# Latent attention: GpSimd subtracts the low halves of the later heads' and the first output projection's weights

## The chip, the cores and the metric

The kernel runs on one core of one Trainium2 chip. A core has a matrix engine (TensorE, PE in the profile, with its weight loads as PEld), three engines for elementwise work (VectorE as DVE, ScalarE as ACT, GpSimd as POOL) and SyncE (SP), which here issues most of the loads. The metric is the device time of one execution in microseconds, taken as the median of several runs. Each engine executes its own instructions strictly in the order in which the program lists them; between engines, semaphores make an instruction wait for the results that it reads and for the buffers that it overwrites.

## The reference

A trunk of two layers on 512 tokens of width 1024, all in float32. Layer 0 mixes with multi-head latent attention (MLA), layer 1 with gated linear attention (GLA); each is followed by an MLP. The change lies in the attention of layer 0. Cut to what matters:

```
h = rms_norm(x) @ w_in                       # latents: 384 for q, 256 for k and v, 64 rotary
q  = rms_norm(c_q)  @ w_uq                   # 8 heads of 128 plain + 64 rotary columns
kv = rms_norm(c_kv) @ w_ukv                  # 8 heads of 128 key columns + 128 value columns
s  = (q_nope k_nope^T + q_rope k_rope^T) * scale, causal
o  = softmax(s) @ v                          # for each head
x  = x + concat(o) @ w_o
```

## The kernel before, in words

Every large product is computed from numbers that are split in two: `hi` is the number rounded to float32r, the form in which TensorE multiplies in one pass, and `lo` is what the rounding left. A product then takes three matmuls (`mm3`, lines 132 to 134): hi by hi, hi by lo, lo by hi. So each piece of weights, once loaded into a buffer `wraw`, costs one ScalarE copy with rounding (`wh`, line 124) and one VectorE subtraction `wl = wraw - wh` (line 127) before TensorE may use the low part. The function `piece` does this; `split` inside it already takes the engine of the subtraction as an argument.

The attention loops over eight heads. `project(h)` makes the plain part of q and k of head h: every fourth head it loads the weights of four heads (three loads `wraw_qn`, two loads `wraw_kn`, lines 580 and 584) and splits the key weights of all four (1024 columns); every second head it splits the query weights of two heads (768 columns). `scores(h)` forms the causal scores and the softmax, `turn` transposes the probabilities and splits them into PTh and PTl (lines 746 and 747), `values` multiplies by v. The loop runs them skewed: in the turn of head h it projects head h+2, transposes h, scores h+1 and multiplies h. The rotary halves of the queries of heads 4 to 7 are computed in the turns of heads 0 and 1 (`rotate_q(t, 1)`): of each such rotation GpSimd does one multiplication (line 624, four in all) and VectorE the rest (lines 623, 625, 626). In the turn of head 6 `out_start` splits the first 256 columns of w_o in two pieces of 1024 and begins the first output projection with heads 0 to 3.

The order of the instructions on each engine is not the order of the code: a scheduler sets it from the dependencies and its own estimates of costs. `afterwards()` asks that the splits of the later heads are issued after line 606 of head 1 (`started`). The buffers limit it too: `wraw` has 2, `wh` and `wl` have 4 each, so a load into `wraw` waits until both halves of the previous piece in that buffer have been formed, and SP issues its loads in order.

In the rows of the order below, a number behind a name is the buffer's own; the profile leaves it out. `wh_879`/`wl_880` are the query weights of heads 2 and 3, `wh_1160`/`wl_1161` the key weights of heads 4 to 7, `wh_1164`/`wl_1165` and `wh_1436`/`wl_1437` the query weights of heads 4, 5 and 6, 7, and `wl_1689`, `wl_1694` the two pieces of w_o. `qh_715`, `kh_728` belong to head 0, `qh_755`, `kh_768` to head 1; `set_773` to `set_776` are the rotated queries of the four token tiles, `tmp_913`, `tmp_919`, `tmp_1048` and `tmp_1054` what GpSimd multiplies for their second half.

Of the kernel before, what the change touches and what calls it, by code (L numbers as in the profile page):

```python
# [18 lines left out]
P = 128  # L19
# [3 lines left out]
ND = D // P  # L23
# [27 lines left out]
def trunk_kernel(ctx: ExitStack, tc: tile.TileContext, t_in: dict, out: bass.AP):  # L51
    nc = tc.nc
    PE, ACT, DVE, POOL, SP = nc.tensor, nc.scalar, nc.vector, nc.gpsimd, nc.sync
# [5 lines left out]
    def uname(s):  # L59
        count[0] += 1  # L60
        return f"{s}_{count[0]}"
# [14 lines left out]
    def bank(tag):  # L76
        return psum["pool"].tile([P, 512], F32, tag=f"ps_{tag}", bufs=psum["banks"][tag], name=uname("ps"))
# [41 lines left out]
    def f(ap):  # L119
        return ap.bitcast(F32)  # L120

    def split(src, hi, lo, hi_eng=ACT, lo_eng=DVE, order=lambda i: i):
        if hi_eng is ACT:
            order(ACT.activation(hi, src, AF.Copy))  # L124
        else:
            hi_eng.tensor_copy(hi, src)
        lo_eng.tensor_tensor(lo, src, f(hi), ALU.subtract)  # L127
# [29 lines left out]
    W_ROOM, W_AT = 1152, 128  # L157
    AT_UP = (124, 60)

    def room_for(tag, a, n, at=W_AT):  # L160
        t = sb.tile([P, W_ROOM], F32R, tag=tag, bufs=4, name=uname(tag))
        return t[:, at : at + a * n].rearrange("p (a n) -> p a n", a=a)

    def piece(raw, a, n, order=lambda i: i, at=(W_AT, W_AT)):
        hi = room_for("wh", a, n, at[0])
        lo = room_for("wl", a, n, at[1])
        split(raw, hi, lo, order=order)
        return hi, lo

    def cut(pair, *idx):  # L170
        return tuple(t[idx] for t in pair)
# [212 lines left out]
    def a_type(psum, w, x, start=True, stop=True, cols=slice(None)):  # L384
        nk = len(x)
        for k in range(nk):
            mm3(psum, cut(w, slice(None), k, cols), x[k], start and k == 0, stop and k == nk - 1)
# [9 lines left out]
    def col_chunk(w2d, c0, n):  # L397
        return load(w2d[:, c0 : c0 + n].rearrange("(k p) n -> p k n", p=P), w2d.shape[0] // P, n)


    def mla(layer, nrm, first, pools):
# [3 lines left out]
        X = nrm.out  # L405
# [34 lines left out]
        raw = sb.tile([P, ND, 256], F32, tag="wraw", bufs=2, name=uname("wraw"))  # L440
# [5 lines left out]
        for j in range(2):  # L446
            p = bank("c")
# [11 lines left out]
        raw = col_chunk(w_in, 256, P)  # L459
        w = piece(raw, ND, P)  # L460
        p = bank("b")
# [5 lines left out]
        raw = col_chunk(w_in, QL + KL, ROPE)  # L467
# [3 lines left out]
        p = bank("b")  # L471
# [23 lines left out]
        raw = sb.tile([P, 2, MH, VD], F32, tag="wraw", bufs=2, name="wraw_v")  # L495
# [18 lines left out]
        for t in range(NT):  # L514
            tk = slice(t * P, (t + 1) * P)
            for hf in range(2):
                p = bank("bc"[hf])
# [15 lines left out]
            if t == 1:  # L533
# [3 lines left out]
                for j in range(2):  # L537
                    y = tmp()
                    DVE.scalar_tensor_tensor(y, pkv[j], gcol("kvn", 2 * layer + j), r_kv, ALU.mult, ALU.mult)
                    hi, lo = (keep.tile([P, S], F32R, tag=f"ckv{j}{x}", name=f"ckv{j}{x}") for x in "hl")  # L540
# [16 lines left out]
        raw = sb.tile([P, 3, MH, ROPE], F32, tag="wraw", bufs=2, name="wraw_qr")  # L557
# [8 lines left out]
        for t in range(NT):  # L566
            tk = slice(t * P, (t + 1) * P)
            p = bank("b")
# [5 lines left out]
        wn, wk = {}, {}  # L574

        def project(h, tag="a"):
            if h % 4 == 0:
                raw = sb.tile([P, 3, 4, NOPE], F32, tag="wraw", bufs=2, name=uname("wraw_qn"))
                for k in range(3):
                    SP.dma_start(raw[:, k], w_uq[:, k, h : h + 4, :NOPE])  # L580
                wn["raw"] = raw
                raw = sb.tile([P, 2, 4, NOPE], F32, tag="wraw", bufs=2, name=uname("wraw_kn"))
                for k in range(2):
                    SP.dma_start(raw[:, k], w_ukv[:, k, h : h + 4, :NOPE])
                with afterwards():
                    wk["p"] = piece(raw.rearrange("p k h c -> p k (h c)"), 2, 512)
            if h % 2 == 0:
                raw = wn["raw"][:, :, h % 4 : h % 4 + 2, :].rearrange("p k h c -> p k (h c)")
                with afterwards():
                    wn["p"] = piece(raw, 3, 256)  # L590
            res = []
            for name, w, c, X_ in (("q", wn["p"], (h % 2) * P, CQ), ("k", wk["p"], (h % 4) * P, CKV)):
                p = bank(tag)
                a_type(p, w, X_, cols=slice(c, c + P))

                c0 = P if name == "q" else 0
                full = keep.tile([P, P], F32, tag=name + "f", bufs=2, name=uname(name + "f"))
                hi, lo = (keep.tile([P, S - c0], F32R, tag=name + x, bufs=2, name=uname(name + x)) for x in "hl")
                if name == "q":
                    ACT.activation(hi, p[:, c0:], AF.Copy, scale=SCALE)  # L600
                    ACT.activation(full, p[:, :P], AF.Copy, scale=SCALE)
                    DVE.scalar_tensor_tensor(lo, p[:, c0:], SCALE, f(hi), ALU.mult, ALU.subtract)
                else:
                    ACT.activation(hi, p, AF.Copy)
                    ACT.activation(full, p[:, :P], AF.Copy)
                    last = DVE.tensor_tensor(lo, p, f(hi), ALU.subtract)
                res.append((hi, lo, full))
            if h == 1:
                started.append(last.ins)
            return res  # L610
# [4 lines left out]
        def afterwards():  # L615
            return tc.issue_after(started[0]) if started else nullcontext()
# [4 lines left out]
        def rotate(dst, src, c, s, shape, eng=DVE):  # L621
# [12 lines left out]
            (P, NT, 2, H),  # L634
        )
        proj = {0: project(0)}


        p = bank("c")[:ROPE]
# [15 lines left out]
        def rotate_q(t, g):  # L655
            rotate(
                QR[t][:, g],
                qs[t].rearrange("p (g h a c) -> p g h a c", g=2, h=HH, a=2)[:, g],
                cos_q[:, t].unsqueeze(1).unsqueeze(1).to_broadcast([P, HH, 2, H]),
                sin_q[:, t].unsqueeze(1).unsqueeze(1).to_broadcast([P, HH, 2, H]),  # L660
                (P, HH, 2, H),
                POOL if g else DVE,
            )


        def turn_q(h):
            p = bank("c")
            for t in range(NT):
                tr(p[:, t * P : (t + 1) * P], QR[t][:, h // HH, h % HH : h % HH + 2].rearrange("p h a c -> p (h a c)"))
            for r in range(2):  # L670
                own, other = slice(r * ROPE, (r + 1) * ROPE), slice((1 - r) * ROPE, (2 - r) * ROPE)
                y = QST[h + r] = slot("B")
                ACT.activation(y[own], p[own], AF.Copy)
                DVE.tensor_tensor(y[other], p[own], f(y[own]), ALU.subtract)
# [54 lines left out]
        O = [None] * MH  # L729
# [25 lines left out]
        def values(h, PT):  # L755
            o = bank("c")
            for j in range(NT):
                vs = slice((h % 4) * VD, (h % 4 + 1) * VD)
                if j < NT - 1:
                    mm3(o[:, j * P :], cut(V[j][h // 4], slice(None), vs), PT[j], j == 0, False)  # L760
                else:
                    PE.matmul(o[:, j * P :], V[j][h // 4][:, vs], PT[j], start=False, stop=True)
            hi, lo = slot("B"), slot("B")
            ACT.activation(hi, o, AF.Copy)
            DVE.tensor_tensor(lo, o, f(hi), ALU.subtract)  # L765
            O[h] = (hi, lo)
# [3 lines left out]
        for h in range(MH):  # L770
            if h + 2 < MH:
                proj[h + 2] = project(h + 2)
            if h < 2:
                with afterwards():
                    for t in (2 * h, 2 * h + 1):
                        rotate_q(t, 1)
            elif h == 2:
                for r in range(HH, MH, 2):
                    turn_q(r)
            if h == MH - 2:  # L780
                begun = out_start(t_in["mla_w_o"][layer], O, 4)
            PT = turn(probs)
            if h + 1 < MH:
                probs = scores(h + 1, *proj[h + 1])
            values(h, PT)
# [2 lines left out]
        return O, begun  # L788


    def out_start(w2d, X, n, tags="aa"):
        raws, w, ps_ = [], [], []
        for m, tag in enumerate(tags):
            if m % 2 == 0:
                raws.append(col_chunk(w2d, m * P, 256))
            w.append(piece(raws[-1][:, :, m % 2 * P : (m % 2 + 1) * P], ND, P))
            ps_.append(bank(tag))

        taken = [0]

        def mms(n=ND):
            for k in range(taken[0], n):
                for p, w_ in zip(ps_, w):
                    mm3(p, cut(w_, slice(None), k), X[k], k == 0, k == ND - 1)
            taken[0] = n

        mms(n)
        return ps_, raws, mms
# [889 lines left out]
    for k0, k1 in ((0, 1), (1, 2), (2, 4), (4, 6), (6, 8)):  # L1698
        w = piece(raw0[:, k0:k1], k1 - k0, KL, tc.keep_in_program_order)
# [9 lines left out]
    O, begun = mla(0, nrm, w0, mla_pools)  # L1709
# [25 lines left out]
    Y, begun = gla(0, n_mix1, "B", "B")  # L1735
# [61 lines left out]
```

## Time and profile before

| What | us |
|---|---|
| Median of 3 runs | 1039.3 (1038.52 to 1039.54) |
| Profiled execution, its own time | 1039.79 |
| Its span in the profile | 1038.1 |
| TensorE busy | 1028.9 (99% of the span) |
| VectorE busy | 879.2 (85%) |
| ScalarE busy | 694.4 (67%) |
| GpSimd busy | 92.7 (9%) |
| Chain of waits: share of TensorE | 92% |
| Chain of waits: share of VectorE | 4% |

The attention's heads lie between about 60 and 150 us of the span. A row of the timeline reads: start, duration, engine, line, operation, output and inputs with their shapes, how many were merged, and in brackets how long the engine had been idle before and what ended that. Matmuls overlap: the next one starts before the profile ends the last, so the distance between starts is what one costs.

### The profile page before, as it was taken

The page shows a single profiled execution, that of the slowest core. Times are in us where ns is not written, and L with a number is a line of the kernel's source. Part 1 is how long each engine was busy: PE and PEld are TensorE (multiplying, and loading weights), DVE is VectorE, ACT ScalarE, POOL GpSimd, SP SyncE. Part 2 cuts the span into 40 slices and gives each one's busy share as a digit, 9 for nine tenths or more (in the row PEclk, how much of TensorE's full clock was granted, in tenths as well). Part 3 has the DMA queues.
Part 4 walks back from the last instruction along what each step waited for, and adds up shares of the span by engine and source line. Part 5 has one row for each costly group of instructions (what it writes and reads, how often), then busy time and mean ns, then how long its engine had stood idle before and what let it go on. Part 6 is the DMA issues. An engine that isn't in the chain of part 4 may idle for free.

```text
span 1038.1 us, 16859 instructions
## 1 busy us (share of the span) xinstructions
PE 1028.9 (99%) x6522; PEld 923.0 (89%) x6522; DVE 879.2 (85%) x1343; ACT 694.4 (67%) x1130; POOL 92.7 (9%) x128
## 2 busy tenths in 40 slices
PE   9999999999999999999999999999999999999997
PEld 7788888899999999998888888888989989989986
DVE  7889976999989989989686399469799999898994
ACT  7667754676776776786445566565677687677784
POOL 7400000400001101000000000000000001100000
PEclk9999999999999999999999999999999999999999
DMA  7501214777677777623312222164568777777422
GB/s 230 127 22 41 73 50 140 205 194 207 189 198 209 169 205 200 157 84 122 90 42 85 91 69 75 48 165 148 144 196 201 189 196 201 192 193 186 121 82 82
DMA packets 63169, 145.85 MB, mean 140 GB/s; under 512 B 9488, under 2 KB 32016, under 8 KB 60528
## 3 DMA queue, kind: packets, MB, share of 16 engines
q1 hardware_dynamic: 52928, 113.57, 33.8%
q0 software_dynamic: 8064, 29.36, 16.4%
q10 hardware_dynamic: 2096, 1.84, 0.6%
q8 instruction: 51, 0.84, 0.3%
q14 instruction: 30, 0.25, 0.1%
HBM read 142.39 MB, written 2.10 MB: 139 GB/s over the span
## 4 chain that ended last, share of the span: by engine, by line
PE 92%; DVE 4%; ACT 2%; DMA 1%; issue 1%; ACTq 0%; SPq 0%; DVEq 0%
PE ps L987 25%; PE ps L1007 13%; PE ps L1000 13%; PE ps L132 10%; PE ps L133 10%; PE ps L134 10%; PE ps L1175 2%; PE ps L149 1%; PE ps L1429 1%; PE ps L1209 1%; PE ps L436 1%; PE ps L1556 1%; DVE wl L127 1%; ACT wh L124 1%; PE ps L1479 0%
## 5 line engine op out<-in xcount | busy, mean ns | idle before, releaser
L124 ACT ACTIVATE wh<-wraw 128x1024 fp32r<-128x1024 f32 x139 | 146.1, 1056 | 113.7 <-PE ps L133 38.4
L127 DVE TENSOR_TENSOR wl<-wraw,wh 128x1024 fp32r<-128x1024 f32 x139 | 169.7, 1222 | 36.5 <-ACT wh L124 35.8
L987 PE MATMUL ps<-T,wh 128*128 128x256 f32 x896 | 154.7, 275 | 0.1
L127 DVE TENSOR_TENSOR wl<-comb,wh 128x1024 fp32r<-128x1024 f32 x112 | 136.6, 1221 | 14.4 <-ACT wh L124 14.4
L124 ACT ACTIVATE wh<-comb 128x1024 fp32r<-128x1024 f32 x112 | 118.6, 1059 | 43.3 <-issue 30.0
L987 PEld LDWEIGHTS ps<-T,wh 128*128 128x128 f32 x896 | 135.0, 188 | 0.4 <-ACT tmp L1017 0.3
L987 PE MATMUL ps<-T,wl 128*128 128x256 f32 x448 | 123.3, 275 | 0.0
L1007 PE MATMUL ps<-wh,set 128*128 128x512 f32 x392 | 122.1, 390 | 0.0
L987 PE MATMUL ps<-set,wh 128*128 128x256 f32 x672 | 116.9, 276 | 0.0
L132 PE MATMUL ps<-set,wh 128*128 128x512 f32 x280 | 109.6, 391 | 0.0
L133 PE MATMUL ps<-set,wh 128*128 128x512 f32 x280 | 109.5, 391 | 0.0
L134 PE MATMUL ps<-set,wl 128*128 128x512 f32 x280 | 109.2, 390 | 0.0
L1000 PE MATMUL ps<-hidden_parts,wh 128*128 128x256 f32 x784 | 105.8, 275 | 0.0
L987 PEld LDWEIGHTS ps<-set,wh 128*128 128x128 f32 x672 | 101.9, 188 | 0.5
L1000 PEld LDWEIGHTS ps<-hidden_parts,wh 128*128 128x128 f32 x784 | 96.6, 188 | 0.0
L987 PE MATMUL ps<-set,wl 128*128 128x256 f32 x336 | 92.5, 275 | 0.0
L1007 PEld LDWEIGHTS ps<-wh,set 128*128 128x128 f32 x392 | 73.6, 188 | 15.2
L987 PEld LDWEIGHTS ps<-T,wl 128*128 128x128 f32 x448 | 84.1, 188 | 0.0
L1007 PE MATMUL ps<-wl,set 128*128 128x512 f32 x196 | 76.3, 389 | 0.0
L987 PEld LDWEIGHTS ps<-set,wl 128*128 128x128 f32 x336 | 63.1, 188 | 0.0
L134 PEld LDWEIGHTS ps<-set,wl 128*128 128x128 f32 x280 | 52.6, 188 | 11.0
L133 PEld LDWEIGHTS ps<-set,wh 128*128 128x128 f32 x280 | 52.6, 188 | 10.9 <-DVE set L765 0.2
(406 smaller groups left out, 2189.5 us busy)
## 6 DMA issues: line engine op xcount, KB each, us to landing
comb<-in_mlp_w_down_dram SPq DMA_DIRECT2D x74, 512.0 KB, 4.2
wraw<-in_mlp_w_up_dram SPq DMA_DIRECT2D x18, 1024.0 KB, 4.9
wraw<-in_mlp_w_up_dram SPq DMA_DIRECT2D x28, 512.0 KB, 5.7
comb<-in_mlp_w_down_dram POOLq DMA_DIRECT2D x28, 512.0 KB, 7.5
wraw<-in_gla_w_in_dram SPq DMA_DIRECT2D x12, 1024.0 KB, 5.1
comb<-in_mlp_w_up_dram SPq DMA_DIRECT2D x14, 512.0 KB, 4.7
comb<-in_mlp_w_up_dram POOLq DMA_DIRECT2D x14, 512.0 KB, 6.7
wraw<-in_mlp_w_up_dram POOLq DMA_DIRECT2D x14, 512.0 KB, 7.3
```

Of the source, the lines that this page charges most:

```text
L124: order(ACT.activation(hi, src, AF.Copy))
L127: lo_eng.tensor_tensor(lo, src, f(hi), ALU.subtract)
L132: PE.matmul(psum, wh, xh, start=start, stop=False)
L133: PE.matmul(psum, wh, xl, start=False, stop=False)
L134: PE.matmul(psum, wl, xh, start=False, stop=stop)
L149: PE.transpose(psum, src, ident[: src.shape[0], : src.shape[0]])
L436: PE.matmul(p, w[:, i, j * P : (j + 1) * P], x, start=start, stop=stop)
L987: PE.matmul(o, a_, x_, start=start and j == 0 and k == 0 and n == 0, stop=k == KH - 1 and n == 2, skip_group_check=True)
L1000: PE.matmul(o, w_[:, k, j * P : (j + 1) * P], x_[:, ts], start=opens, stop=k == 1 and n == 2, skip_group_check=True)
L1007: PE.matmul(o, x_, w_, start=start and k == 0 and n == 0, stop=k == 1 and n == 2, skip_group_check=True)
L1175: PE.matmul(p, a, x, start=k == 0 and n == 0, stop=k == 3 and n == 2)
L1209: PE.matmul(o, a, b_, start=False, stop=k == 3 and n == 2, skip_group_check=True)
```

## The change

`piece` gets an argument `lo_eng` and hands it to `split`. For the key weights of heads 4 to 7, the query weights of heads 2 to 7 and the two first pieces of w_o the subtraction is issued on GpSimd. Those of head 0, and all other pieces of the program, stay on VectorE. No number that is computed changes.

```diff
-    def piece(raw, a, n, order=lambda i: i, at=(W_AT, W_AT)):
+    def piece(raw, a, n, order=lambda i: i, at=(W_AT, W_AT), lo_eng=DVE):
         hi = room_for("wh", a, n, at[0])
         lo = room_for("wl", a, n, at[1])
-        split(raw, hi, lo, order=order)
+        split(raw, hi, lo, lo_eng=lo_eng, order=order)
...
-                    wk["p"] = piece(raw.rearrange("p k h c -> p k (h c)"), 2, 512)
+                    wk["p"] = piece(raw.rearrange("p k h c -> p k (h c)"), 2, 512, lo_eng=POOL if h else DVE)
...
-                    wn["p"] = piece(raw, 3, 256)
+                    wn["p"] = piece(raw, 3, 256, lo_eng=POOL if h else DVE)
...
-                begun = out_start(t_in["mla_w_o"][layer], O, 4)
+                begun = out_start(t_in["mla_w_o"][layer], O, 4, lo_eng=POOL)
...
-    def out_start(w2d, X, n, tags="aa"):
+    def out_start(w2d, X, n, tags="aa", lo_eng=DVE):
...
-            w.append(piece(raws[-1][:, :, m % 2 * P : (m % 2 + 1) * P], ND, P))
+            w.append(piece(raws[-1][:, :, m % 2 * P : (m % 2 + 1) * P], ND, P, lo_eng=lo_eng))
```

The scheduler answers with another order on every engine but SP. The first place is ScalarE, between the last copy of the rotary queries and the evacuation of head 0's q and k. Before:

```order
L572 ACTIVATE set_680<-ps_670 128x512
L600 ACTIVATE qh_715<-ps_704 128x384
L601 ACTIVATE qf_714<-ps_704 128x128
L604 ACTIVATE kh_728<-ps_720 128x512
L605 ACTIVATE kf_727<-ps_720 128x128
L644 ACTIVATE KB<-ps_733 64x512
L645 ACTIVATE KA<-ps_733 64x512
L600 ACTIVATE qh_755<-ps_744 128x384
```

Now:

```order
L572 ACTIVATE set_680<-ps_670 128x512
L124 ACTIVATE wh_1160<-wraw_kn_1157 128x1024
L600 ACTIVATE qh_715<-ps_704 128x384
L601 ACTIVATE qf_714<-ps_704 128x128
L604 ACTIVATE kh_728<-ps_720 128x512
L605 ACTIVATE kf_727<-ps_720 128x128
L644 ACTIVATE KB<-ps_733 64x512
L645 ACTIVATE KA<-ps_733 64x512
L124 ACTIVATE wh_1164<-wraw_qn_1153 128x768
L600 ACTIVATE qh_755<-ps_744 128x384
```

The two roundings for heads 4 to 7 stood behind line 605 of head 2 (`kf_906`); they now stand ahead of the evacuations of head 0 and of head 1.

The second place is GpSimd, from the end of the rotary tables to the first load that it issues for the MLP. Before:

```order
L369 TENSOR_SCALAR rope_turns<-rope_236 128x128
L624 TENSOR_TENSOR tmp_913<-set_644,rope_tabs_q 128x256
L624 TENSOR_TENSOR tmp_919<-set_656,rope_tabs_q 128x256
L624 TENSOR_TENSOR tmp_1048<-set_668,rope_tabs_q 128x256
L624 TENSOR_TENSOR tmp_1054<-set_680,rope_tabs_q 128x256
L976 DMA comb_2343<-in_mlp_w_up_dram 128x1024
```

Now:

```order
L369 TENSOR_SCALAR rope_turns<-rope_236 128x128
L127 TENSOR_TENSOR wl_880<-wraw_qn_689,wh_879 128x768
L127 TENSOR_TENSOR wl_1161<-wraw_kn_1157,wh_1160 128x1024
L127 TENSOR_TENSOR wl_1165<-wraw_qn_1153,wh_1164 128x768
L624 TENSOR_TENSOR tmp_913<-set_644,rope_tabs_q 128x256
L624 TENSOR_TENSOR tmp_919<-set_656,rope_tabs_q 128x256
L624 TENSOR_TENSOR tmp_1048<-set_668,rope_tabs_q 128x256
L127 TENSOR_TENSOR wl_1437<-wraw_qn_1153,wh_1436 128x768
L624 TENSOR_TENSOR tmp_1054<-set_680,rope_tabs_q 128x256
L127 TENSOR_TENSOR wl_1689<-wraw_1686,wh_1688 128x1024
L127 TENSOR_TENSOR wl_1694<-wraw_1686,wh_1693 128x1024
L976 DMA comb_2343<-in_mlp_w_up_dram 128x1024
```

Six subtractions are added, three of 768 and three of 1024 columns, and the rotary multiplications now stand behind some of them.

The third place is VectorE in the turn of head 1, from line 606 of head 3 to the splits of head 1's probabilities. Before:

```order
L606 TENSOR_TENSOR kl_1043<-ps_1034,kh_1042 128x512
L625 TENSOR_TENSOR set_775<-tmp_1047,tmp_1048 128x4x32
L626 TENSOR_TENSOR set_775<-tmp_1047,tmp_1048 128x4x32
L623 TENSOR_TENSOR tmp_1053<-set_680,rope_tabs_q 128x256
L747 TENSOR_TENSOR PTl_1065<-ps_1059,PTh_1064 128x512
L625 TENSOR_TENSOR set_776<-tmp_1053,tmp_1054 128x4x32
L626 TENSOR_TENSOR set_776<-tmp_1053,tmp_1054 128x4x32
L747 TENSOR_TENSOR PTl_1073<-ps_1068,PTh_1072 128x384
```

Now:

```order
L606 TENSOR_TENSOR kl_1043<-ps_1034,kh_1042 128x512
L625 TENSOR_TENSOR set_775<-tmp_1047,tmp_1048 128x4x32
L626 TENSOR_TENSOR set_775<-tmp_1047,tmp_1048 128x4x32
L623 TENSOR_TENSOR tmp_1053<-set_680,rope_tabs_q 128x256
L704 TENSOR_TENSOR ps_1086<-ps_1086,causal 128x2x128
L625 TENSOR_TENSOR set_776<-tmp_1053,tmp_1054 128x4x32
L626 TENSOR_TENSOR set_776<-tmp_1053,tmp_1054 128x4x32
L747 TENSOR_TENSOR PTl_1065<-ps_1059,PTh_1064 128x512
L747 TENSOR_TENSOR PTl_1073<-ps_1068,PTh_1072 128x384
```

The two instructions that read `tmp_1054` moved from behind the first split of the probabilities to ahead of it. In the same turn the rounding `wh_1688` of w_o moved up on ScalarE to directly behind `wh_1436`, ahead of `PTh_1064`.

## The prediction

> **What bounds the kernel now.** I read the busy times first, then the windows of the attention (columns: stretch, its length, busy us and count of PE, PEld, DVE, ACT, POOL, granted clock, DMA share, GB/s), then who waited for whom between 60 and 150 us.
>
> ```profile
> PE 1028.9 (99%) x6522; PEld 923.0 (89%) x6522; DVE 879.2 (85%) x1343; ACT 694.4 (67%) x1130; POOL 92.7 (9%) x128
> ...
> 70.00:80.00 10.00, 9.75 (x54) 8.12 (x53) 9.79 (x32) 7.76 (x20) 0.76 (x1) 1.00 0.19 54
> 80.00:90.00 10.00, 10.00 (x59) 8.79 (x58) 10.00 (x36) 6.46 (x18) 0.00 (x0) 1.00 0.00 1
> ...
> sum 90.00, PE 89.54 PEld 75.82 DVE 79.90 ACT 58.55 POOL 3.01; mean PE 9.95 PEld 8.42 DVE 8.88 ACT 6.51 POOL 0.33
> ...
> PEld ps L692 <- ACT pr L143: 1.4, 3, 0.6
> PEld ps L149 <- DVE pr L726: 1.0, 4, 0.3
> PEld ps L132 <- DVE PTl L747: 0.6, 2, 0.4
> PEld ps L149 <- DVE PTl L747: 0.4, 1, 0.4
> PEld ps L762 <- ACT PTf L751: 0.3, 1, 0.3
> PEld ps L695 <- DVE kl L606: 0.2, 1, 0.2
> PEld ps L698 <- DVE set L674: 0.2, 1, 0.2
> ```
>
> TensorE bounds it. VectorE is full too in the turns of heads 0 to 3, but over the 90 us TensorE itself is idle for 0.46 us, and its weight loads waited 4.1 us in all for VectorE and ScalarE. So even if every wait vanished, the change could win 4.1 us; what it can lose has no such bound, since each new wait of TensorE counts in full.
>
> **What the six subtractions cost on GpSimd.** No row has one of this size there, so I take the rows beside it.
>
> ```profile
> 37.78 0.46 POOL L352 TENSOR_TENSOR rope<-rope,rope 128x128 f32<-128x128 f32 x1
> 62.83 0.73 POOL L624 TENSOR_TENSOR tmp<-set,rope_tabs_q 128x256 f32<-128x256 f32 x1 [0.50 <-DVE set L626]
> ...
> 69.46 0.96 DVE L127 TENSOR_TENSOR wl<-wraw_qn,wh 128x768 fp32r<-128x768 f32 x1
> 45.90 1.23 DVE L127 TENSOR_TENSOR wl<-wraw_kn,wh 128x1024 fp32r<-128x1024 f32 x1 [0.65 <-ACT wh L124]
> ```
>
> From 128 to 256 columns a two-input operation grows from 0.46 to 0.73 us: 0.27 us for each 128, and 0.19 at the start. That gives 0.73 + 4 x 0.27 = 1.8 us for 768 and 0.73 + 6 x 0.27 = 2.35 us for 1024. The bounds: VectorE's own 0.96 and 1.23 below, and 3 x 0.73 = 2.2 and 4 x 0.73 = 2.9 above. I take 1.8 and 2.35. [...] VectorE is rid of 3 x 0.96 + 3 x 1.23 = 6.6 us of work.
>
> **The two engines block each other.** The profile shows it where rotary work of both overlapped.
>
> ```profile
> 27.65 1.48 DVE L127 TENSOR_TENSOR wl<-wraw_v,wh 128x1024 fp32r<-128x1024 f32 x1
> ...
> 59.51 0.28 DVE L625 TENSOR_TENSOR set<-tmp,tmp 128x128 f32<-128x128 f32 x1
> 61.77 0.71 DVE L625 TENSOR_TENSOR set<-tmp,tmp 128x128 f32<-128x128 f32 x1
> 64.14 0.69 DVE L606 TENSOR_TENSOR kl<-ps,kh 128x512 fp32r<-128x512 f32 x1 [0.91 <-ACT kf L605]
> ...
> 61.56 0.78 POOL L624 TENSOR_TENSOR tmp<-set,rope_tabs_q 128x256 f32<-128x256 f32 x1 [22.47 <-DVE set L626]
> 64.25 0.74 POOL L624 TENSOR_TENSOR tmp<-set,rope_tabs_q 128x256 f32<-128x256 f32 x1 [0.69 <-ACT kf L605]
> ```
>
> Line 625, with both inputs in SBUF, takes 0.28 us alone and 0.71 us beside the GpSimd operation of 61.56: it ends at 62.48, 0.14 us behind it. Line 127 takes 1.48 instead of 1.23 us. Line 606, which reads PSUM and one SBUF tensor, keeps its 0.69 us beside the operation of 64.25. So a VectorE instruction with two SBUF inputs waits until GpSimd's has read its inputs, and those that read PSUM don't. How long a 1024-wide one holds VectorE off no row shows; I take all of it but the 0.19 us at the start, 2.2 us, with 0 as the other bound.
>
> **Term 1: ScalarE waits for a load ahead of head 0 (60 to 75 us).** In the new order `wh_1160` stands ahead of head 0's `qh_715`, and its weights must have landed by then.
>
> ```profile
> 57.25 0.85 ACT L124 ACTIVATE wh<-wraw_qn 128x768 fp32r<-128x768 f32 x1
> 61.98 0.49 ACT L600 ACTIVATE qh<-ps 128x384 fp32r<-128x384 f32 x1 [1.44 <-PE ps L134]
> 63.34 0.60 ACT L604 ACTIVATE kh<-ps 128x512 fp32r<-128x512 f32 x1 [0.70 <-PE ps L134]
> 65.86 0.49 ACT L600 ACTIVATE qh<-ps 128x384 fp32r<-128x384 f32 x1 [0.67 <-PE ps L134]
> 76.83 1.10 ACT L124 ACTIVATE wh<-wraw_kn 128x1024 fp32r<-128x1024 f32 x1
> ...
> 70.50 0.92 SPq L584 DMA_DIRECT2D wraw_kn<-in_mla_w_ukv_dram  x2
> DMA to landing us min/median/max: 2.9/3.2/3.4
> ...
> 66.63 0.56 DVE L602 SCALAR_TENSOR_TENSOR ql<-ps,qh 128x384 fp32r<-128x384 f32 x1
> 68.02 0.69 DVE L606 TENSOR_TENSOR kl<-ps,kh 128x512 fp32r<-128x512 f32 x1 [0.83 <-ACT kf L605]
> 70.45 1.41 DVE L674 TENSOR_TENSOR set<-ps,set 64x512 fp32r<-64x512 f32 x2
> 71.78 0.61 DVE L704 TENSOR_TENSOR ps<-ps,causal 128x256 f32<-128x256 f32 x2
> ...
> 67.60 0.36 PE L695 MATMUL ps<-kh,qh 128*128 128x256 f32 x1
> 74.92 0.38 PE L692 MATMUL ps<-kf,qf 128*128 128x128 f32 x1 [0.16 <-ACT pr L143]
> ```
>
> `wh_879` ends at 57.25 + 0.85 = 58.1. `wl_880` on GpSimd then ends at about 60.1 (1.8 us and up to 0.3 behind VectorE's rotations, which in turn are held up 1.6 us; they have that slack, the transposes that read them come after 67). Only then may SP issue the two key loads into that buffer, as it did at 70.50, when `wl_880` had ended at 70.42 on VectorE. The second follows about 0.4 us behind and lands 3.3 us later: 64.0. `wh_1160` runs to 65.1, and `qh_715` starts at about 65.0 instead of 61.98. From there to head 1's `qh_755` ScalarE worked 65.86 - 61.98 - 0.70 - 0.67 = 2.5 us, plus 0.8 now for `wh_1164`: it starts at 68.25, 2.4 us late. VectorE's `ql` follows it by 0.77 us and lasts 0.56: 69.6. TensorE waits for that at the row of 67.60, in whose PSUM bank head 1's q lies: about 2 us.
>
> Next on VectorE: `kl` of head 1 starts 2.16 us behind `qh_755`, less the 0.70 us that ScalarE no longer waits: 69.7, and the copy of line 674 behind it ends at 71.1. Between that and line 704 there were `wl_880` and two of line 674, 71.78 - 69.43 = 2.35 us; without `wl_880` 1.4. Added are two of line 623 and one of line 625, 0.9 us by the distance of their starts; they read what GpSimd forms only behind `wl_1161` (65.1 to 67.5) and `wl_1165` (from 68.3, the end of `wh_1164`, to 70.1), and each can be held off by a line 624, 0 to 1.1 us in all. Line 704 comes at 73.4 to 74.5, **1.6 to 2.7 us late**, with the softmax of head 0 behind it. At 74.92 TensorE already waited for that softmax, so the delay stands there whole. I take **+2.3 us**.
>
> **Term 2: the splits of head 1's probabilities wait for GpSimd (86 to 94 us of the old clock).**
>
> ```profile
> 84.71 0.39 PE L134 MATMUL ps<-ckv1h,wl 128*128 128x512 f32 x1
> 86.43 0.90 ACT L124 ACTIVATE wh<-wraw_qn 128x768 fp32r<-128x768 f32 x1
> 88.17 0.68 DVE L747 TENSOR_TENSOR PTl<-ps,PTh 128x512 fp32r<-128x512 f32 x1
> 89.34 0.39 PE L132 MATMUL ps<-PTh,set 128*128 128x512 f32 x1
> ```
>
> I count on from here as if term 1 had shifted every row alike. Head 3's k leaves TensorE at 85.1; its two copies and `wh_1436` end at 86.7 at the earliest (87.33 before). GpSimd's order makes `wl_1437` 86.7 to 88.5, `tmp_1054` to 89.2, then `wl_1689`, whose rounding has ended by then, to 91.6. VectorE's order puts everything that reads `tmp_1054` ahead of PTl. Without blocking PTl would start at 89.2 + 0.4 and end at 90.3. With it the first line 625 (ready at 87.0) waits for `wl_1437`, line 626 for `tmp_1054`, line 623 for `wl_1689` until 91.7; then come 623, 704, 625, 626, 1.1 us by their starts, and PTl ends at about 93.4. TensorE gets to PTl at about 89.2 (89.34, less the one matmul that stood ahead of it and now doesn't). The wait is **1.1 to 4.3 us**. I take **+4.0 us**, nearer to the upper end, as the rows at 61.77 and 27.65 show blocking both ways.
>
> **Term 3: the rest, heads 2 to 7.** VectorE has 6.6 us less to do, which can take away the waits of the first list; about 2.5 of the 4.1 us lie after 90 us. Against that the new order transposes probabilities as soon as they should be ready, with fewer matmuls ahead, and moves the last pieces of w_o on VectorE ahead of head 5's PTl; each can add some tenths. Bounds -2.5 and +1.5; I take **0**. `wl_1689` and `wl_1694` themselves are used after 131 us and are hidden. All behind the attention keeps its order and shifts.
>
> **The sum** is 2.3 + 4.0 + 0 = 6.3 us on the profiled execution's 1039.79, so 1046.1; that one ran 0.5 us above the median of 1039.3, against which I forecast 1045.5.
>
> **The rivals.** (a) *GpSimd's operations don't hold VectorE off for their length.* Then terms 1 and 2 are 1.6 and 1.1: 1042.0. For it speaks only that no long one is in the trace. [...] (b) *The relief wins.* If the key weights land before 61 us and `tmp_1054` comes before TensorE wants PTl, terms 1 and 2 vanish and the waits for VectorE go: at 80 to 90 us VectorE is busy 10.00 of 10. Half of 4.1 us: 1037.2. It decides if `wl_880` ends by 57, which its input forbids. (c) *The wait of term 2 costs clock as well.* In no window above was less than 1.00 granted, and no wait there was longer than 0.6 us. At half clock, the matmuls from 89.34 to about 91.05 would take 1.7 us more: 1047.2. [...] (d) *No change*: TensorE's queue hides both waits. It is full, so hardly.
>
> **How the numbers follow.** Forecast 60%, (a) 20%, (b) 7%, (c) 7%, (d) 6%. The forecast's own range is 1043.5 to 1048; with (a) and most of (c), and 1.6 + 1.1 - 1 at the low end, the range is 1041.0 to 1048.5. About 0.2%, 2 us, can be told from no change: slower 84%, within 10%, faster 6%.
>
> **What would show it.** ScalarE idle from 60.5 to about 64 ahead of line 124 for the key loads; `qh` of head 0 near 65; TensorE waiting 2 us near 67.6; GpSimd's line 127 at 1.8 and 2.35 us; lines 625, 626 and 623 of VectorE stretched to 1 or 2 us near 90, and TensorE waiting 4 us for PTl. If ScalarE doesn't idle at 61, or lines 623 to 626 keep 0.28 to 0.42 us beside line 127 of GpSimd, the forecast is wrong.

## The result, and the profile after

The changed kernel takes 1047.3 us (median of six runs, 1046.83 to 1047.69) against 1039.3 us before, measured beside it on the same chip: a ratio of 1.0077, 95% interval 1.0067 to 1.0087. It is 8.0 us slower. The forecast was 1045.5 with a range of 1041.0 to 1048.5, and slower at 84%. The profiled execution took 1047.15 us with a span of 1045.4.

First the busy times of the page and the windows of the attention (columns as before: stretch, length, busy us and count of PE, PEld, DVE, ACT, POOL, then the granted clock, DMA share and GB/s).

```profile
PE 1029.9 (99%) x6522; PEld 925.0 (88%) x6522; DVE 880.5 (84%) x1337; ACT 695.2 (66%) x1130; POOL 105.2 (10%) x134
...
70.00:80.00 10.00, 8.82 (x52) 7.38 (x50) 9.76 (x30) 5.61 (x16) 1.57 (x2) 1.00 0.12 39
...
90.00:100.00 10.00, 6.11 (x21) 4.97 (x20) 9.32 (x24) 3.16 (x11) 3.38 (x3) 0.69 0.34 105
...
sum 90.00, PE 82.78 PEld 71.46 DVE 76.31 ACT 54.83 POOL 13.84; mean PE 9.20 PEld 7.94 DVE 8.48 ACT 6.09 POOL 1.54
```

VectorE has lost six instructions that cost 6.6 us before, and yet it is busy 880.5 us instead of 879.2. The time in which an instruction is held off counts as busy in this view (rows below), so those 880.5 hold about 7.9 us more of waiting than before (880.5 - 879.2 + 6.6). TensorE is idle for 7.2 of the 90 us instead of 0.46, and from 90 to 100 us it was granted 0.69 of its clock, where every window before had 1.00.

The longest waits of TensorE and the one of ScalarE that starts the first of them, between 58 and 155 us (us in total, times, longest):

```profile
PEld ps L132 <- DVE PTl L747: 4.9, 3, 4.3
ACT wh L124 <- DMA wraw_kn<-in_mla_w_ukv_dram: 3.5, 1, 3.5
PEld ps L695 <- DVE ql L602: 1.8, 1, 1.8
PEld ps L692 <- ACT pr L143: 1.4, 1, 1.4
```

To add up what TensorE lost, I took for each of its matmuls the distance to the start of the next, less the usual distance for its width (0.227 us for 512 columns, 0.177 for 384, 0.113 for 256, 0.108 for 128, the medians of the trace). One product in float32r is one matmul in the trace (line 695: 24 for 24 in eight heads), one in float32 of lines 692 and 762 two (16 for eight heads each). Summed by stretches of each execution's own span, in us:

| Stretch | before | after | difference |
|---|---|---|---|
| 60 to 80 | 1.30 | 3.76 | +2.5 |
| 80 to 90 | 0.17 | 0.45 | +0.3 |
| 90 to 100 | 0.66 | 6.57 | +5.9 |
| 100 to 150 | 2.42 | 1.90 | -0.5 |
| all | 4.55 | 12.68 | +8.1 |

Of the 6.57 us, 4.06 are one wait (90.77 + 0.23 to 95.05) and 2.5 are matmuls behind it at half rate. The profiled executions themselves differ by 7.36 us: the changed one reached the last copy of the rotary queries 0.86 us earlier (59.08 against 59.94), so its times up to there are 0.86 us below the ones in the prediction.

**Where the first 2.5 us are.** The issue of the key loads on SP, the rounding and head 0's and head 1's q on ScalarE, then VectorE's lines 624, 623 and 704:

```profile
59.38 0.92 SPq L584 DMA_DIRECT2D wraw_kn<-in_mla_w_ukv_dram  x2
...
63.21 1.06 ACT L124 ACTIVATE wh<-wraw_kn 128x1024 fp32r<-128x1024 f32 x1 [3.54 <-DMA wraw_kn<-in_mla_w_ukv_dram]
64.18 0.47 ACT L600 ACTIVATE qh<-ps 128x384 fp32r<-128x384 f32 x1
67.31 0.47 ACT L600 ACTIVATE qh<-ps 128x384 fp32r<-128x384 f32 x1
...
57.58 2.07 DVE L624 TENSOR_TENSOR tmp<-set,rope_tabs_q 128x256 f32<-128x256 f32 x1
70.07 1.79 DVE L623 TENSOR_TENSOR tmp<-set,rope_tabs_q 128x256 f32<-128x256 f32 x2
73.42 0.61 DVE L704 TENSOR_TENSOR ps<-ps,causal 128x256 f32<-128x256 f32 x2
```

ScalarE stands still for 3.54 us until the keys have landed; behind it wait q and k of head 0, which TensorE had ready. Line 704, with which head 0's softmax begins, comes at 73.42, which is 74.28 on the clock of before, where it was at 71.78.

**Where the wait of 4 us is.** GpSimd's instructions, then VectorE's ahead of PTl of head 1, then TensorE at it:

```profile
57.31 2.04 POOL L127 TENSOR_TENSOR wl<-wraw_qn,wh 128x768 fp32r<-128x768 f32 x1 [19.05 <-DVE tmp L624]
64.35 2.40 POOL L127 TENSOR_TENSOR wl<-wraw_kn,wh 128x1024 fp32r<-128x1024 f32 x1 [5.00 <-ACT wh L124]
88.44 1.85 POOL L127 TENSOR_TENSOR wl<-wraw_qn,wh 128x768 fp32r<-128x768 f32 x1 [16.86 <-PE ps L149]
90.24 0.79 POOL L624 TENSOR_TENSOR tmp<-set,rope_tabs_q 128x256 f32<-128x256 f32 x1
90.99 2.39 POOL L127 TENSOR_TENSOR wl<-wraw,wh 128x1024 fp32r<-128x1024 f32 x1
```

```profile
88.52 1.91 DVE L625 TENSOR_TENSOR set<-tmp,tmp 128x128 f32<-128x128 f32 x1
90.35 0.83 DVE L626 TENSOR_TENSOR set<-tmp,tmp 128x128 f32<-128x128 f32 x1
91.10 2.56 DVE L623 TENSOR_TENSOR tmp<-set,rope_tabs_q 128x256 f32<-128x256 f32 x1
93.92 0.28 DVE L625 TENSOR_TENSOR set<-tmp,tmp 128x128 f32<-128x128 f32 x1
94.32 1.47 DVE L747 TENSOR_TENSOR PTl<-ps,PTh 128x512 fp32r<-128x512 f32 x3
...
90.77 0.40 PE L699 MATMUL ps<-KB,set 128*128 128x512 f32 x1
95.05 0.79 PE L132 MATMUL ps<-PTh,set 128*128 128x512 f32 x1 [3.89 <-DVE PTl L747]
95.64 0.63 PE L133 MATMUL ps<-PTl,set 128*128 128x512 f32 x1
98.95 0.63 PE L133 MATMUL ps<-cq0l,wh 128*128 128x512 f32 x1
```

Each of three VectorE instructions starts behind a GpSimd instruction and ends 0.14 to 0.28 us after it: line 625 at 90.43 behind 90.29, line 626 at 91.18 behind 91.03, line 623 at 93.66 behind 93.38. As soon as GpSimd is quiet, line 625 takes its 0.28 us. In the last two rows a matmul of 512 columns lasts 0.63 us instead of 0.39, and the next one starts 0.43 us later instead of 0.23. The granted clock is 0.50 from 93.71 to 100.54 us; TensorE works again from 95.05, so it runs at half rate for about 5.5 us.

### The profile page after: what moved, and what is told of

Its sections match the earlier page's. It is cut to its first block, busy times and chain, and to the rows that moved or that the text cites. A ratio compares the mean times of both kernels' runs of the same rounds, so it can differ in the third digit from the quotient of the medians.

```text
span 1045.4 us, 16864 instructions
## 1 busy us (share of the span) xinstructions
PE 1029.9 (99%) x6522; PEld 925.0 (88%) x6522; DVE 880.5 (84%) x1337; ACT 695.2 (66%) x1130; POOL 105.2 (10%) x134
## 4 chain that ended last, share of the span: by engine, by line
PE 90%; DVE 6%; ACT 3%; issue 1%; DMA 1%; ACTq 0%; SPq 0%; DVEq 0%
PE ps L987 24%; PE ps L1007 13%; PE ps L1000 13%; PE ps L132 10%; PE ps L133 10%; PE ps L134 10%; PE ps L1175 2%; PE ps L1429 1%; PE ps L1209 1%; PE ps L149 1%; PE ps L436 1%; PE ps L1556 1%; DVE wl L127 1%; ACT wh L124 1%; PE ps L1479 0%
## 5 line engine op out<-in xcount | busy, mean ns | idle before, releaser
L127 DVE TENSOR_TENSOR wl<-wraw,wh 128x1024 fp32r<-128x1024 f32 x137 | 166.9, 1220 | 37.6 <-ACT wh L124 36.9
```

## The experiments

In the experiments but two the order of all engines in the attention is that of the changed kernel, with only the named rows moved. It was held by dependencies that set the order of issue alone and no wait, one from each instruction to the one behind it on its engine:

```python
for a, b in zip(order, order[1:]):
    tc.add_manual_dep(
        traced[b], traced[a].name,
        mybir.DependencyInfo(mybir.DependencyClass.NoSync, mybir.DependencyReason.DATA),
        reason="pin",
    )
```

Two theories stood against each other throughout: that the loss is the sum of a load that ScalarE waits for, of GpSimd holding VectorE off, and of a lower clock behind the wait; and that it is the new order by itself. Each run was measured against the kernel before on the same chip, in five rounds. Two runs were not made: none keeps the six subtractions on VectorE in the new order, so what the order alone costs is not measured, and none holds the changed order with nothing moved. For the latter stand the rows of experiment 1 ahead of its added matmuls, which start within 0.15 us of the changed kernel's (line 625 at 88.62 against 88.52).

**1. TensorE kept busy through the wait.**

```diff
-                a_type(p, w, X_, cols=slice(c, c + P))
+                [PE.matmul(p, w[0][:, 0, c : c + P], X_[0][0]) for _ in range(17 if h == 4 and name == 'q' else 0)]; a_type(p, w, X_, cols=slice(c, c + P))
```

> The order of every engine in the attention is that of the changed kernel; only TensorE gets 17 more matmuls (the first one of head 4's q, written 17 times more into its own empty bank, where the real one then starts afresh) right ahead of the first matmul on head 1's probabilities, where it stood still for 4.06 us. At 0.227 us each they fill 3.9 us and are useless work. Theory (the pause of TensorE itself costs the clock, 2.7 us): granted clock 1.00 from 90 to 110 us instead of 0.69 and 0.97, the matmuls behind the wait at 0.23 us distance instead of 0.43, and the time falls by 2.7 us to 1044.5 (1044.0 to 1045.2), though work is added. Rival (the low clock comes from what the other engines do there, not from the pause): 0.69 again, and 1047.0 or more.

Measured: 1045.2 us (1044.67 to 1046.79), ratio 1.0060 (1.0047 to 1.0074): 2.1 us less than the changed kernel in the medians, with 17 matmuls more. Four of the five runs lie below every run of the changed kernel; the fifth, 1046.79, lies just under its fastest. A window and TensorE's rows at the place:

```profile
90.00:100.00 10.00, 9.93 (x48) 8.06 (x47) 9.79 (x27) 4.12 (x14) 3.53 (x3) 1.00 0.34 105
...
91.12 4.01 PE L594 MATMUL ps<-cq0h,wh 128*128 128x512 f32 x17
95.54 0.39 PE L133 MATMUL ps<-PTl,set 128*128 128x512 f32 x1
```

The granted clock is 1.00, from 100 to 110 us too, and the matmul behind takes 0.39 us again, while GpSimd's subtractions and VectorE's held rows are the ones of the changed kernel. So the low clock comes from TensorE's own pause. It costs some 2 to 2.5 us: 2.1 by the medians, 2.5 by the sum of lost time in the profiled executions (12.68 against 6.34 and 17 x 0.227).

**2. The first w_o piece taken out of the way.** On ScalarE:

```diff
 L124 ACTIVATE wh_1436<-wraw_qn_1153 128x768
-L124 ACTIVATE wh_1688<-wraw_1686 128x1024
 L746 ACTIVATE PTh_1064<-ps_1059 128x512
...
 L605 ACTIVATE kf_1191<-ps_1184 128x128
+L124 ACTIVATE wh_1688<-wraw_1686 128x1024
```

> As the changed kernel, with one instruction moved: ScalarE's rounding of the first w_o piece goes from ahead of head 1's PTh to behind head 4's copies of k (about 104 us), so GpSimd's subtraction of that piece (2.39 us at 90.99) leaves the place where VectorE's rotations stand. Theory (the 2.56 us of VectorE's line 623 are 2.1 us of blocking by that subtraction): line 623 back at 0.4 to 0.6 us, PTl 2.1 us earlier, TensorE's wait 1.9 instead of 4.06 us; if a wait of that length doesn't touch the clock, 2.1 + 2.7 less: 1042.4 (1041.8 to 1043.2); if the clock loss goes with the length of the wait, 1043.8. Rival (no blocking: VectorE only waits in order for GpSimd's product of the rotation): line 623 and the wait stay, 1047.

Measured: 1043.7 us (1043.32 to 1043.93), ratio 1.0042 (1.0030 to 1.0055). VectorE's line 623 and the waits of TensorE from 85 to 110 us:

```profile
91.56 0.41 DVE L623 TENSOR_TENSOR tmp<-set,rope_tabs_q 128x256 f32<-128x256 f32 x1
...
PE ps L132 <- DVE PTl L747: 1.7, 1, 1.7
PE ps L149 <- DVE PTl L747: 1.1, 1, 1.1
```

Line 623 is back at 0.41 us, so 2.15 of its 2.56 us were that one subtraction. The pause for PTl shrinks to 1.89 us (the distance of starts, 2.12, less 0.23), and the clock stays at 1.00 in every window. The time is the 1043.8 named for a partial loss of clock, but for another reason: the clock came back whole, and TensorE now stands for 1.1 us at the transposes of head 2's probabilities.

**3. PTl ahead of the blocked rotations.** On VectorE the three rows `PTl_1065`, `PTl_1073`, `PTl_1081` (line 747) go from behind the second line 626 to directly behind `kl_1043` (line 606).

> As the changed kernel, with three instructions moved: VectorE takes head 1's three PTl ahead of the rotations that wait for GpSimd, instead of behind them. Theory (PTl reads PSUM and isn't blocked; its place in VectorE's queue makes the wait): PTl at 88.6 with its 0.68 us although GpSimd's 768-wide subtraction runs beside it, no wait of TensorE there, granted clock 1.00, 4.06 + 2.7 us less: 1040.4, and up to 1.5 us more where head 2's softmax, still behind the blocked rotations, comes late for TensorE in its turn: 1040.2 to 1042.0. Rival (what reads PSUM is blocked too by a long GpSimd operation): PTl stretched to over 1.5 us, and 1044 or more.

Measured: 1043.6 us (1043.52 to 1044.29), ratio 1.0044 (1.0031 to 1.0056), 1.6 us above the theory's range and just under the rival's. PTl on VectorE, TensorE at the next waits and behind them, and one window:

```profile
90.23 1.49 DVE L747 TENSOR_TENSOR PTl<-ps,PTh 128x512 fp32r<-128x512 f32 x3 [1.21 <-ACT PTh L746]
...
98.73 0.33 PE L149 MATMUL ps<-ident,pr 128*128 128x128 f32 x1 [1.02 <-DVE set L765]
101.17 0.53 PE L698 MATMUL ps<-KA,set 128*128 128x384 f32 x1
...
100.00:110.00 10.00, 9.68 (x49) 8.37 (x49) 9.02 (x25) 6.33 (x17) 0.00 (x0) 0.83 0.01 2
```

PTl reads PSUM and takes its 1.49 us for three although GpSimd subtracts beside it (88.84 to 90.69, then from 91.34): not blocked, and TensorE no longer waits there. But head 2's softmax stands behind the rotations that are blocked, TensorE loses 2.0 us between 95 and 100, and then 1.9 us more up to 105, most of it to a granted clock of 0.83. I had not expected the clock to fall for waits of 1.2 and 0.6 us so close together.

**4. ScalarE without its wait for the keys.** On ScalarE and on GpSimd:

```diff
 L572 ACTIVATE set_680<-ps_670 128x512
-L124 ACTIVATE wh_1160<-wraw_kn_1157 128x1024
 L600 ACTIVATE qh_715<-ps_704 128x384
...
-L124 ACTIVATE wh_1164<-wraw_qn_1153 128x768
 L600 ACTIVATE qh_755<-ps_744 128x384
...
 L673 ACTIVATE set_873<-ps_868 64x512
+L124 ACTIVATE wh_1160<-wraw_kn_1157 128x1024
 L673 ACTIVATE set_876<-ps_868 64x512
+L124 ACTIVATE wh_1164<-wraw_qn_1153 128x768
...
 L127 TENSOR_TENSOR wl_880<-wraw_qn_689,wh_879 128x768
-L127 TENSOR_TENSOR wl_1161<-wraw_kn_1157,wh_1160 128x1024
-L127 TENSOR_TENSOR wl_1165<-wraw_qn_1153,wh_1164 128x768
 L624 TENSOR_TENSOR tmp_913<-set_644,rope_tabs_q 128x256
 L624 TENSOR_TENSOR tmp_919<-set_656,rope_tabs_q 128x256
 L624 TENSOR_TENSOR tmp_1048<-set_668,rope_tabs_q 128x256
+L127 TENSOR_TENSOR wl_1161<-wraw_kn_1157,wh_1160 128x1024
+L127 TENSOR_TENSOR wl_1165<-wraw_qn_1153,wh_1164 128x768
```

> As the changed kernel, with the key weights of heads 4 to 7 and the query weights of heads 4 and 5 rounded later on ScalarE (behind the copies of head 2's rotary part, at about 70 us, instead of ahead of head 0's q), and GpSimd's two subtractions behind its three rotary products. Theory (term 1: ScalarE waits 3.5 us for the key load ahead of head 0's q): ScalarE's qh at 61.1 and 65.0 us, no wait of TensorE at 66.6, line 704 at 70.9 instead of 73.4, everything behind 2.5 us earlier, the wait for PTl and the low clock behind it as before: 1044.7 (1044.0 to 1045.4). Rival (the 2.5 us come from VectorE, whose rotations GpSimd holds up): the first row of line 704 stays near 73, and 1046.5 to 1047.5.

Measured: 1047.8 us (1046.74 to 1048.76), ratio 1.0082 (1.0068 to 1.0096): nothing won. Head 0's q on ScalarE, GpSimd's two subtractions, and VectorE's rotation and softmax of head 0 (this execution runs 0.36 us behind the changed one at the start):

```profile
61.48 0.49 ACT L600 ACTIVATE qh<-ps 128x384 fp32r<-128x384 f32 x1 [1.44 <-PE ps L134]
...
71.19 2.40 POOL L127 TENSOR_TENSOR wl<-wraw_kn,wh 128x1024 fp32r<-128x1024 f32 x1 [6.18 <-ACT wh L124]
73.54 1.82 POOL L127 TENSOR_TENSOR wl<-wraw_qn,wh 128x768 fp32r<-128x768 f32 x1
...
68.95 0.76 DVE L623 TENSOR_TENSOR tmp<-set,rope_tabs_q 128x256 f32<-128x256 f32 x2
71.28 0.61 DVE L704 TENSOR_TENSOR ps<-ps,causal 128x256 f32<-128x256 f32 x2
72.60 1.02 DVE L709 TENSOR_TENSOR stat<-stat,cols 128x1 f32<-128x1 f32 x1
73.87 1.51 DVE L709 TENSOR_TENSOR stat<-stat,cols 128x1 f32<-128x1 f32 x1
```

That ScalarE's wait made head 0's q late and TensorE wait near 66.7 us is shown: q and line 704 come when the theory said (61.48 and 71.28, less 0.36, are 61.1 and 70.9), and up to 73.5 us TensorE loses no more than before (0.32 us). The rival is not excluded as a part: the edit also took GpSimd's two subtractions away from VectorE's rotations, and two of line 623 took 0.76 us here against 1.79 in the changed kernel. So how much of the 2.5 us at line 704 was the wait, and how much the hold, the run does not tell. What it would have won was lost again two rows further on. Line 709 multiplies one column by one column, both in SBUF, and takes 0.15 us; here it takes 1.02 and 1.51, and ends 0.02 to 0.03 us behind the two subtractions, which now fall into the softmax. Neither theory had named that. TensorE then waits 2.1 us for head 0's softmax and is granted 0.90 from 70 to 80 us.

**5. The order of before, the engines of the change.** TensorE, ScalarE and VectorE issue the attention as the kernel before did, VectorE without the six; GpSimd does the subtraction for heads 2 and 3 ahead of its rotary products and the other five behind them.

> The six subtractions run on GpSimd as in the change, but TensorE, ScalarE and VectorE issue everything in the attention in the order of the kernel before (VectorE without the six); GpSimd takes each subtraction as its rounding comes, behind its four rotary products. Theory (a GpSimd subtraction holds off every VectorE instruction that reads two SBUF tensors, so also in the old order): ScalarE no longer waits ahead of head 0's q, but the key and query subtractions of heads 4 and 5 run from about 78 to 82 us, hold lines 625, 626, 623 and 709 of VectorE for 1.8 to 2.4 us, and TensorE waits about 2 us for PTl of head 0; wl of heads 6 and 7 at 87 to 89 us does the like to head 1, and the w_o pieces at 102 to 107 us hold line 709 of head 3's softmax: 3 to 7 us over before, 1043.5 (1041.5 to 1046.5). Rival (the new order makes the loss, not the engine): 1039.5 or less, since VectorE has 6.6 us less to do.

Measured: 1045.8 us (1044.72 to 1047.4), ratio 1.0063 (1.0051 to 1.0076). The held-off rows of VectorE, and TensorE at the first wait and behind it:

```profile
79.68 2.45 DVE L626 TENSOR_TENSOR set<-tmp,tmp 128x128 f32<-128x128 f32 x1
90.57 1.95 DVE L625 TENSOR_TENSOR set<-tmp,tmp 128x128 f32<-128x128 f32 x1
109.56 1.89 DVE L709 TENSOR_TENSOR stat<-stat,cols 128x1 f32<-128x1 f32 x1
...
82.78 0.50 PE L132 MATMUL ps<-PTh,set 128*128 128x512 f32 x1 [1.88 <-DVE PTl L747]
85.95 0.63 PE L133 MATMUL ps<-cq2l,wh 128*128 128x512 f32 x1
```

The rival falls: with the old order the kernel is still 6.4 us slower than before, at the three places that were named, the third some 4 us later than named. So moving the work alone makes 6.4 of the 8.0 us. In the medians the new order costs 0.14% more than the old one with the same engines (ratios 1.0077 and 1.0063), but the two intervals overlap, so that difference is not shown.

**6. All three moves around head 1's probabilities.** VectorE as in experiment 3, ScalarE as in 2, and on GpSimd the last rotary product goes ahead:

```diff
 L624 TENSOR_TENSOR tmp_1048<-set_668,rope_tabs_q 128x256
+L624 TENSOR_TENSOR tmp_1054<-set_680,rope_tabs_q 128x256
 L127 TENSOR_TENSOR wl_1437<-wraw_qn_1153,wh_1436 128x768
-L624 TENSOR_TENSOR tmp_1054<-set_680,rope_tabs_q 128x256
```

> As the changed kernel, with the three moves around head 1's probabilities together: VectorE takes its three PTl ahead of the last rotations, ScalarE rounds the first w_o piece only behind head 4's copies of k, and GpSimd forms its last rotary product ahead of the subtraction for heads 6 and 7. Theory (the loss is a sum: term 1 of 2.5 us, the wait for PTl of 4.06 us, 2.5 us of clock behind it, and about 1.1 us won elsewhere): no wait over 1 us from 85 to 105 us, granted clock 1.00 all through, term 1 as before, so 1047.2 - 4.06 - 2.5 = 1040.6 (1040.0 to 1041.5). Rival (a blocked VectorE instruction only moves the loss on to head 2's softmax, as in the run with PTl first): 1042.5 to 1044.

Measured: 1041.8 us (1041.35 to 1042.3), ratio 1.0025 (1.0015 to 1.0035), 0.3 us above the theory's range and under the rival's. The clock is 1.00 in all windows; one wait of 1.1 us for PTl is left near 99 us, which I had not counted; it would make most of the difference to 1040.6. From 60 to 80 us TensorE loses 3.71 us, as in the changed kernel (3.76). Without the second wait and its clock the kernel keeps 2.4 us over before, and term 1 alone is 2.4 us (3.71 - 1.30). So the parts add up, but only in sum: from 80 to 100 us TensorE still loses 1.0 us more than before, the wait included, and from 100 to 150 us it loses 1.0 us less (1.44 against 2.41).

**7. Three of the six, where VectorE reads PSUM.** The order of before; `wl_880`, `wl_1689` and `wl_1694` on GpSimd, the other three on VectorE. On ScalarE `wh_1688` goes from behind `PTh_1232` to behind `kf_1336`, and `wh_1693` from behind `qf_1323` to behind `kf_1463`.

> The order of the kernel before on all engines, with only three subtractions on GpSimd: the query weights of heads 2 and 3, and the two first w_o pieces, whose roundings ScalarE does behind the copies of head 5's and head 6's k, so that GpSimd's 2.4 us fall where VectorE's instructions read PSUM (PTl, lines 602, 606, 704), not in a softmax. Keys of heads 4 to 7 and queries of heads 4 to 7 stay on VectorE. Theory (a subtraction beside instructions that read PSUM costs VectorE nothing): VectorE is rid of 0.96 + 1.22 + 1.21 us, head 0's softmax comes up to 0.96 us earlier, no new wait of TensorE: 1038.8 (1038.0 to 1039.5), 0.5 us under before. Rival (GpSimd's work always costs VectorE as much as it takes off): 1040 or more.

Measured: 1038.55 us (1037.82 to 1038.86, eleven runs), ratio 0.9992 (0.9984 to 1.0001): 0.8 us under before in the medians, with an interval that just reaches 1, so a gain is likely but not shown. The rival, 1040 or more, falls. GpSimd and VectorE beside each other:

```profile
116.34 2.40 POOL L127 TENSOR_TENSOR wl<-wraw,wh 128x1024 fp32r<-128x1024 f32 x1 [5.64 <-ACT wh L124]
...
116.83 0.56 DVE L602 SCALAR_TENSOR_TENSOR ql<-ps,qh 128x384 fp32r<-128x384 f32 x1 [0.34 <-PE ps L699]
117.67 1.49 DVE L747 TENSOR_TENSOR PTl<-ps,PTh 128x512 fp32r<-128x512 f32 x3 [0.28 <-ACT PTh L746]
```

The same subtraction of 2.40 us costs VectorE nothing where its instructions read PSUM: three PTl take 1.49 us beside it, 1.47 in the changed kernel with GpSimd quiet. TensorE's lost time from 60 to 150 us is 4.0 us against 4.55 before: even placed well, there is little to win, because VectorE was hardly the bound. Of all the kernels run this is the fastest.

**8. The subtractions in pieces.** Line numbers are higher by 8 here (623 is 631, 625 is 633).

```diff
-        lo_eng.tensor_tensor(lo, src, f(hi), ALU.subtract)
+        [lo_eng.tensor_tensor(lo[s_], src[s_], f(hi)[s_], ALU.subtract) for s_ in cuts(lo_eng, lo)]
```

(`cuts` gives slices of 256 columns on GpSimd, the whole on VectorE.)

> As the changed kernel, in its order on every engine; only each GpSimd subtraction is issued in pieces of 256 columns (three for 768, four for 1024). A piece should take some 0.7 us, so GpSimd works 0.3 to 0.4 us longer on each. Theory (VectorE is held off by one GpSimd instruction at a time and comes in between two): the lines 625, 626 and 623 ahead of head 1's PTl last 0.7 to 0.8 us each instead of 1.91, 0.83 and 2.56, line 624 near 57 us 0.8 instead of 2.07; PTl comes 1.5 us earlier, at about 92.9, TensorE waits 2.6 us instead of 4.06, and what of the clock comes back with it is open: 1045.7 with none, 1043.2 with all of it; 1044.5. Rival (VectorE gets in only when GpSimd has no more work): those rows as long as before or longer, 1047.2 to 1048.

Measured: 1046.3 us (1045.09 to 1047.07), ratio 1.0065 (1.0053 to 1.0077), 0.6 us above what the theory gave at the most and under the rival. Two of VectorE's rows and the wait:

```profile
90.37 0.80 DVE L633 TENSOR_TENSOR set<-tmp,tmp 128x128 f32<-128x128 f32 x1
91.86 0.96 DVE L631 TENSOR_TENSOR tmp<-set,rope_tabs_q 128x256 f32<-128x256 f32 x1
...
PE ps L140 <- DVE PTl L755: 2.6, 1, 2.6
```

The hold is that of one GpSimd instruction: behind pieces of a third it is 0.80 us instead of 1.91, behind pieces of a quarter 0.96 instead of 2.56. But now five instructions ahead of PTl are held instead of three, TensorE still waits 2.76 us (distance of starts less 0.23), and from 96.63 to 100.05 us the granted clock is again 0.50. Cutting won 1.0 us in the medians, with intervals that overlap; choosing the place won 5.5 us in experiment 6 and 8.7 in experiment 7, the latter in the order of before and with three of the six back on VectorE.

## Why the prediction was right, and where it was not

- **The bound.** Right: TensorE, with at most 4.1 us to win. Experiment 7, the best placing found, won 0.8 in the medians.
- **GpSimd's prices.** 1.8 and 2.35 us were taken, 1.83 to 2.04 and 2.39 to 2.41 measured in the changed kernel.
- **The engines block each other.** Right, and rival (a) with it wrong: of a 1024-wide subtraction line 623 was held 2.15 us (2.56 - 0.41), where 2.2 was taken. The rule as I put it, "a VectorE instruction with two SBUF inputs waits", holds down to one column (experiments 4 and 5), which I had not thought through: I looked only at the rotations and never at line 709. Line 709 takes 0.15 us alone and 1.02, 1.51 and 1.89 beside GpSimd's subtractions there. Every held row above reads two SBUF tensors; PTl, which reads PSUM and one SBUF tensor, was not held (1.49 us for three in experiment 3, 1.47 in the changed kernel with GpSimd quiet). Measured of the end of a hold is that the held instruction ends 0.02 to 0.30 us behind GpSimd's (changed kernel, experiments 4 and 5); that GpSimd's reading of its inputs sets it was my estimate from the 0.14 us in the trace of before.
- **Term 1.** The mechanism was right as far as it was tried, and its size nearly so: 2.3 forecast, 2.5 measured (2.4 by experiment 6). Its two parts, the wait for the load and the hold of the rotations, were not measured apart. With 0.86 us added, `wh_1160` came at 64.07 (64.0 forecast), `qh_715` at 65.04 (65.0), `qh_755` at 68.17 (68.25), line 704 at 74.28 (73.4 to 74.5).
- **Term 2.** Right: 4.0 us forecast, 4.06 measured. On the count of the prediction the first PTl ended at 93.4 (95.0 + 0.86 - 2.5), the forecast time.
- **The clock.** Here the forecast failed. I had it as rival (c), 7% and 1.7 us, and it came on top of the forecast case. Two steps were wrong. The chance: from 60 to 150 us of the trace of before no wait was longer than 0.6 us and the clock stayed at 1.00, so nothing showed how long a wait must be to cost clock, and the 7% were my estimate alone. In the step of 3.41 us before the fall, 90.30 to 93.71, TensorE was idle for 2.73 us, and the last section shows falls after 2.0 us. A wait of 4.0 us puts at least 2.0 of them into one step wherever it starts, so by these traces, as an estimate, it costs clock at nearly every position, and the loss belonged to the likeliest case. The price: half rate itself stood in the trace of before (granted 0.50 from 1034.8 us to the end), but I let it last for the matmuls of head 1's values only, some 1.7 us; TensorE ran at it for about 5.5 us, and it cost 2.7 (2.50 up to 100 us and 0.18 behind).
- **Term 3.** Forecast 0, measured about -1.1: 8.1 less 2.5, 4.06 and 2.7. Why it is below nothing was not tried; the long wait may cover small ones of before at 90 to 120 us. It hid part of the clock's loss, so that the forecast is only 1.8 us short. That the time fell within the range is to that extent luck: two misses, of 2.7 and of -1.1 us, partly cancelled.
- **Rivals (b) and (d)** did not happen: `wl_880` ended at 59.35, the keys landed at 63.2, and TensorE's queue hid neither wait.

## What to carry to other kernels

Work on an idle engine is not free if it holds off a busy one: before moving an operation to GpSimd, list what VectorE does in that stretch, and count each instruction with two SBUF inputs, however small, as held until GpSimd's instruction ends (here line 709 went from 0.15 us to 1.89, line 623 from 0.41 to 2.56). Put such work beside instructions that read PSUM (three PTl took 1.49 us beside it in experiment 3, 1.47 alone), and look at what the scheduler moves in answer, loads behind buffers above all. And where TensorE's pauses add up to some 2 us within one step of 3.41 us, price the matmuls at half rate that may follow: here 1.6 us behind a pause of 2.04 (experiment 5), 2.7 behind one of 4.06, and behind others nothing.

## What the runs showed of the hardware that was not expected

**The clock falls for pauses of about 2 us, and not each time.** Half rate followed pauses of 4.06 us (changed kernel, and once more in experiment 4), 2.76 (8), 2.14 and then 0.6 (4), 2.04 (5), and of 1.2 and 0.6 us in close succession (3). It did not follow pauses of 2.36 us near 68 us (8), 1.89 near 92 us (2) and 2.06 near 110 us (5).

The traces show what divides them. In each of them the granted clock changes only at instants a whole number of 3.41 us apart (in experiment 4 at 78.05, 81.46, 95.11 and 101.94), and half rate lasts one such step, or two behind the pauses of 4.06 us. Experiment 5 around its pause, step by step (columns as above):

```profile
80.26:83.67 3.41, 1.53 (x7) 0.95 (x6) 3.41 (x6) 0.11 (x1) 3.41 (x2) 1.00 0.17 46
83.67:87.08 3.41, 3.41 (x13) 3.12 (x12) 3.41 (x15) 1.97 (x6) 0.14 (x1) 0.50 0.77 264
87.08:90.50 3.42, 3.42 (x23) 3.09 (x23) 2.32 (x8) 3.35 (x9) 0.00 (x0) 1.00 0.00 0
```

TensorE's lost time, summed step by step over all ten traces from 10 us on and reckoned as in the table of the result, is 2.02 to 2.86 us in the six steps that a fall follows (the fall at the end of each kernel left out), and at most 2.00 us in every other step at full rate. So here the idle time within one step decided, not the length of a pause: of the 2.36 us in experiment 8, 1.38 lie on one side of a boundary and 0.98 on the other, of the 2.06 us in experiment 5 0.74 and 1.32, while its 2.04 us lie within one step. Nor was the step before a fall idle as a whole: TensorE was busy for 1.53 of the 3.41 us in experiment 5 and for 0.87 in the changed kernel. This is read from the traces afterwards; no run was made to test where the limit lies. The boundaries lie elsewhere in each trace (the first full clock begins 4.96 us behind the start of the span in the changed kernel, 5.83 in experiment 6), so a given pause can cost clock in one execution and not in the next.

The same kernel varies too: the changed kernel's four runs with a mean granted clock of 0.995 took 1047.15 to 1047.69, the two with 0.997 took 1046.83 and 1046.90; in experiment 5 the runs with 0.999 took 1044.72 and 1044.93, those with 0.997 1045.3 to 1046.4 and the one with 0.995 1047.4. Not all spread is the clock's: experiment 1's five runs, all at 0.998 or 0.999, took 1044.67 to 1046.79.

**Useless work can pay.** In experiment 1 seventeen matmuls whose result nobody reads made the kernel 2.1 us faster than the changed one, in the medians.
